# Attention scores by each head's own 64 rows, two weight granules multiplied unsplit, and six raw buffers, in a two-layer float32 decoder trunk

## The chip, the cores and the metric

The kernel runs on one core of one Trainium2 chip. The metric is the device time of one execution in microseconds (us). Three executions of the kernel before took 739.08, 737.74 and 739.0 us, so the median is 739.0 us.

TensorE multiplies: a weight load puts a stationary operand of up to 128 rows (the contraction) by 128 columns into the array, and a matmul streams a moving operand of up to 512 columns past it; sums go to PSUM banks. VectorE (DVE), ScalarE (ACT) and GpSimd (POOL) do the elementwise work, and SyncE's queue (SP) issues the DMA transfers, one after the other. Each engine executes its own instructions in the order of the program and waits on semaphores for the others.

## The reference, cut to what matters

One sequence of 256 tokens, 1024 features, passes two layers, all in float32. Per layer:

```python
proj = x @ w_in          # q,k,v of 8 stick-breaking heads | q,k,v of 8 MoBA heads | two gates
q_sb, k_sb, v_sb, q_mb, k_mb, v_mb, g_sb, g_mb = jnp.split(proj, cuts, axis=-1)
# stick-breaking, per head of 64 features:
z = jnp.einsum('bhqd,bhkd->bhqk', qi, k).astype(jnp.float32) * scale
log_keep = jnp.where(past, jax.nn.log_sigmoid(-z), 0.0)
suffix = lax.cumsum(log_keep, axis=3, reverse=True) - log_keep
w = jnp.where(past, jnp.exp(jax.nn.log_sigmoid(z) + suffix), 0.0)
# MoBA with rope on q and k; with 256 tokens only the own block is left: causal softmax
merged = jax.nn.sigmoid(g_sb) * branch_sb + jax.nn.sigmoid(g_mb) * branch_mb
x = layer_norm(DEEPNORM_ALPHA * x + merged @ w_out, ln_mix_g[l], ln_mix_b[l])
x = layer_norm(DEEPNORM_ALPHA * x + swiglu(x, w_gate, w_up, w_down), ln_ffn_g[l], ln_ffn_b[l])
```

In both kinds of attention a score is a product over the 64 features of one head, for each pair of a query and an earlier key.

## The kernel before, in words

**Precision.** Matmuls work on the type float32r, which keeps a part of float32's bits. To come near float32, each operand is split into a high part (a cast to float32r on ACT) and a low part (the rest, by a subtraction on DVE), and a product is three matmuls that add into one bank: high by high, high by low, low by high (`mm3`, line 334).

**Weights.** All weights come in granules of 128 by 1024 float32 (512 KB), 122 for each layer, in the order of their use. `WeightStream.load` (line 132) issues a granule's DMA into one of `NRAW` = 4 raw buffers; the first granule goes in two halves. `WeightStream.line` (line 143) casts it into a ring of ten granules (`whi`, ACT, line 162) and subtracts (`wlo`, DVE, line 166); then the raw buffer is free for a later granule, whose DMA the SP queue issues. `take` (line 175) hands a split granule to the matmuls.

**Order.** The order of all instructions is written out while the program is built. `Weave` keeps a planned time for TensorE (`weave.t`), ACT and DVE; a generator for a side task (splitting weights, a head pair's attention, rope) is stepped when the plan says that its next input is there. Each `mm` advances the plan by `max(n, 256) / 2400.0 + 0.002` us. The plan decides where a side task's matmuls and transposes stand among the others in TensorE's order; what really happens on the chip follows that order, whether inputs are there or not.

**Start.** Seven matmuls on zeros (`N_WARM`) are issued first. The input, transposed (`xT`), comes in eight pieces of 128 KB between the first granules, and is split into `xT_hi` and `xT_lo`. Layer 0 then begins with two projections of 128 tokens by 512 columns, twice each: values of the stick-breaking heads (`l0pv`, granules 0 to 3) and queries of the MoBA heads (`l0pq`, granules 4 to 7). `both_tokens` (line 368) runs them in an order of (token half, granule). Their sums stand in the two banks of pool `psM`. After `l0pq`, each token half goes through `rope_line`: a copy on ACT, rope on DVE, four transposes on TensorE (`l0qmb_tp`), and `put_qmb`.

**Scores.** Two heads make a pair: 64 rows each of one 128-row tile. For the queries, `stack_q` (line 401) makes a tile per head: its 64 rows hold the high part, the other 64 rows the low part. For the keys, `twice_k` (line 411) makes a tile per head with the high part in both halves, and another with the low part in the head's rows and zeros (a POOL memset) in the others. Then two matmuls over all 128 rows give a head's scores. The core of `scores` (line 449) is

```python
mm(o, q[h][:, p0 + j, qs], kh[h][:, p0 + j, ks], True, False)
mm(o, q[h][:, p0 + j, qs], kl[h][:, p0 + j, ks], False, True)
```

for two pairs, two heads and two query blocks (128 queries by 128 keys, 128 by 256): 16 matmuls in a group. There are four groups a layer (`sb0`, `sb1`, `mb0`, `mb1`), eight in all. The scores of a pair fill a tile of pool `psB` with one bank for each head; the transposed weights (`pT`) use the same pool, and `turnB` lets one line of attention at a time have it.

**Units.** Most large activations share `NACT` = 13 buffers of 4 KB a partition.

Of the kernel before, what the change touches and what calls it, by code (L numbers as in the profile page):

```python
# [31 lines left out]
EARLY = [*range(8), 8, 14, 9, 15, 20, 24, 21, 25, *range(10, 14), *range(16, 20), 22, 23, *range(26, 40)]  # L32
NACT = 13
NWIDE = 4
# [65 lines left out]
class WeightStream:  # L100
# [3 lines left out]
    def __init__(self, nc, pool, w, total, weave, rings):  # L104
        self.nc, self.pool, self.w, self.total, self.weave = nc, pool, w, total, weave
        self.loaded = self.split = 0
        self.done = -1
        self.current = 0
        self.rings = rings
        self._lay()  # L110
        self.dma_t = 1.7
        self.raw, self.parts, self.there, self.ready = {}, {}, {}, {}
# [14 lines left out]
    def _pieces(self, g):  # L127
        n = 2 if g == 0 else 1
        c = GCOLS // n
        return [slice(i * c, (i + 1) * c) for i in range(n)]  # L130

    def load(self, upto):
        while self.loaded < min(upto, self.total):
            g = self.loaded
            t = self.pool.tile([P, GCOLS], F32, tag="raw", name=f"raw{g}", bufs=NRAW)
            for sl in self._pieces(g):
                self.nc.sync.dma_start(t[:, sl], self.w[place(g), :, sl])
            self.raw[g] = t
# [45 lines left out]
RING = 10 * GCOLS + LINES  # L184
NRAW = 4
NSPLIT = 10
HOLD = 8
N_WARM = 7
LEAD = 2
# [21 lines left out]
def hybrid_trunk_kernel(ctx: ExitStack, tc: tile.TileContext, w, xT_in, x_in, ln_in,  # L211
# [57 lines left out]
    ident = const.tile([P, P], F32, name="ident")  # L269
    sb_kl = const.tile([P, 2, 2, S], F32R, name="sb_kl")  # L270
    ends = const.tile([P, 384], F32, name="ends")
    mask = const.tile([P, 2, P], F32, name="mask")
    warm = small.tile([P, 1], F32, tag="nmu", name="warm")

    nc.gpsimd.memset(sb_kl.bitcast(F32), 0.0)
    nc.gpsimd.memset(ends, 0.0)
# [11 lines left out]
    def load_xT(t, ks):  # L288
        nc.sync.dma_start(xT_raw[t][:, ks, :], xT_in[:, t, ks, :])
# [6 lines left out]

    kcs = [slice(k, k + 2) for k in range(0, KC, 2)]
    ws.side = weave.add(ws.line(), last=True)
    load_xT(0, kcs[0])
    ws.load(1)  # L300
    load_xT(1, kcs[0])
    for i in range(1, 4):
        load_xT(0, kcs[i])
        ws.load(i + 1)
        load_xT(1, kcs[i])
    split_xT(0, kcs[0])
    ws.take(0)
    split_xT(1, kcs[0])
    for i in range(1, 4):
        split_xT(0, kcs[i])  # L310
        if i < 3:
            ws.take(i)
        split_xT(1, kcs[i])
    weave.t = 4.5
# [12 lines left out]
    def mm(o, a, b, start, stop):  # L327
        nc.tensor.matmul(o, a, b, start=start, stop=stop)  # L328
        n = 1
        for d in b.shape[1:]:  # L330
            n *= d
        weave.t += max(n, 256) / 2400.0 + 0.002

# [21 lines left out]
    def split_to(hi, lo, src, n):  # L355
        return weave.start(split_line(hi, lo, src, n, pe_done()))

    def tok_major(o, g, t, first, last, k0):

        hi, lo = ws.take(g)  # L360
        hi = hi.rearrange("p (k c) -> p k c", k=2)
        lo = lo.rearrange("p (k c) -> p k c", k=2)
        for k in range(2):
            ts = slice(t * P, (t + 1) * P)
            mm3(o, xT_hi[:, k0 + k, ts], xT_lo[:, k0 + k, ts], hi[:, k, :], lo[:, k, :],
                first and k == 0, last and k == 1)

    def both_tokens(name, g0, put):

        acc = [bankM(f"{name}{t}", [P, WIDTH]) for t in range(2)]  # L370
        order = ((0, 0), (1, 0), (0, 1), (1, 1), (0, 2), (0, 3)) if g0 == 0 else \
            ((0, 0), (0, 1), (0, 2), (1, 0), (1, 1), (0, 3))
        for t, k in order + ((1, 2), (1, 3)):
            tok_major(acc[t], g0 + k, t, k == 0, k == 3, 2 * k)
            if t == 1:
                ws.used(g0 + k)
            if k == 3:
                put(t, acc[t])
# [17 lines left out]

    ROWS = [(slice(h * DH, (h + 1) * DH), slice((1 - h) * DH, (2 - h) * DH)) for h in range(2)]

    def stack_q(qs, src, n, c, e):

        for h, (a, b) in enumerate(ROWS):
            e = act(e, n, nc.scalar.activation, qs[h][a], src[a], AF.Copy, scale=c)
        yield e
        for h, (a, b) in enumerate(ROWS):
            e = dve(e, n, nc.vector.scalar_tensor_tensor, qs[h][b], src[a], c, qs[h][a].bitcast(F32),
                    op0=OP.mult, op1=OP.subtract)
        return e

    def twice_k(kh, kl, src, n, e):

        for h, (a, b) in enumerate(ROWS):
            e = act(e, n, nc.scalar.copy, kh[h][a], src[a])
        yield e
        e2 = e
        for h, (a, b) in enumerate(ROWS):
            e2 = dve(e2, n, nc.vector.tensor_sub, kl[h][a], src[a], kh[h][a].bitcast(F32))
            e = act(e, n, nc.scalar.copy, kh[h][b], kh[h][a].bitcast(F32))
        return max(e, e2)  # L420

# [26 lines left out]

    def scores(name, q, kh, kl, m, p0):
# [36 lines left out]
    def product_line(name, p, parts, v, oT, e, due):  # L486
# [19 lines left out]
        yield e  # L506
        for h, (a, b) in enumerate(ROWS):
            e = dve(e, S, nc.vector.tensor_add, both[a], o[:DH, h, :], low[:DH, h, :])
        yield e
        yield from split_line(oT[0][:, p, :], oT[1][:, p, :], both, S, e)  # L510

    def sb_line(name, d, q, q_there, ps, v, oT, done):

        kh = work.tile([P, 2, 2, S], F32R, tag="sbkh", name=f"{name}kh")
        kh, kl = ([x[:, h] for h in range(2)] for x in (kh, sb_kl))
# [5 lines left out]
        ss, es = yield from scores(name, q, kh, kl, 0, 0)  # L521
        ws_, fs = [], []
# [18 lines left out]

    def mb_line(name, d, q, kh, kl, v, oT, before, done, scored):
        while len(before) < 2:
# [4 lines left out]
        scored.append(name)  # L548
        ss, es = yield from scores(name, q, kh, kl, 1, 2 * d)
        work_, fs = [], []  # L550
# [111 lines left out]
    for l in range(DEPTH):  # L662
# [4 lines left out]
        v_sb = v_parts(L + "vsb")  # L667
        q_mb = [unit(f"{L}qmb{h}", [P, NPAIR, S], F32R) for h in range(2)]

        def put_qmb(tp, ts, e):  # L670
            return stack_q([q[:, :, ts] for q in q_mb], tp, WIDTH, 0.125, e)

# [30 lines left out]
        def sb_pairs(d, g):  # L703
            q = work.tile([P, 2, 2, S], F32R, tag="sbq", name=f"{L}sbq{d}")
            q, there = [q[:, h] for h in range(2)], [0.0]

            def q_line(ps):
                there[0] = 1e9
                there[0] = yield from stack_q(q, ps, WIDTH, 0.125, pe_done())
# [24 lines left out]
        sb_pairs(1, G + 12)  # L734
        k_mb = [[unit(f"{L}kmb{n}{h}", [P, NPAIR, S], F32R) for h in range(2)] for n in range(2)]
        for h, (a, b) in enumerate(ROWS):
            nc.gpsimd.memset(k_mb[1][h][b].bitcast(F32), 0.0)
# [9 lines left out]
        for d in range(2):  # L747
            sides.append(weave.add(mb_line(f"{L}mb{d}", d, q_mb, *k_mb, v_mb, o_mb, sigmoids, exps, scored)))
        for c in range(1, KC):
# [198 lines left out]
```

## Time and profile before

| what | before |
|---|---|
| median of three executions | 739.0 us |
| the profiled execution | 739.39 us |
| its span, first to last instruction | 737.4 us |
| PE busy | 724.9 us, 98% |
| PE weight loads busy | 670.1 us, 91% |
| DVE busy | 530.4 us, 72% |
| ACT busy | 408.0 us, 55% |
| DMA | 136.32 MB, mean 185 GB/s |

The profile is one execution. PE is TensorE's matmuls, PEld its weight loads, which run beside them. A row of a timeline gives the start and the duration in us, then engine, line, operation, output and inputs, the shape and how many were merged; brackets give the idle time before and what ended it. Matmuls overlap each other, so the pace of a stream is the distance of the starts, not the duration of one. Line L328 is the helper in which every matmul is issued, L341 the transposes', L51 and L56 the helpers of ACT and DVE, L137 the DMA of a granule.

### The profile page before, as it was taken

Reading aid. Unit: us, or ns where it says so; the run is one execution under the profiler, and the core shown is the slowest. Engines: PE = TensorE matmul, PEld = TensorE weight load, DVE = VectorE, ACT = ScalarE, POOL = GpSimd, SP = SyncE. Lnnn points to the kernel's source line nnn. Section 1 sums busy time; section 2 is a strip of 40 time slices with the busy share of each in tenths; the row PEclk is TensorE's granted clock in tenths of the full one; section 3 lists DMA queues with packets and bytes.
Section 4 is the critical chain, followed back from the end, with each engine's and each line's share of the span. In section 5 each row is a group of like instructions: output and inputs, shape, how many; then the busy total and the mean of one; then the engine's idle time right before and its main releaser. Section 6 shows DMA issues by size and latency. Waiting matters only on the chain.

```text
span 737.4 us, 12709 instructions
## 1 busy us (share of the span) xinstructions
PE 724.9 (98%) x5081; PEld 670.1 (91%) x5081; DVE 530.4 (72%) x740; ACT 408.0 (55%) x603; POOL 19.5 (3%) x35
## 2 busy tenths in 40 slices
PE   8999999999999999999999999999999999999996
PEld 6798899998799999988889989999988999999885
DVE  6798968796886666644479888778878866655416
ACT  6686767744565545534257856777446655444400
POOL 0001000000000000000000100000010000000001
PEclk9999999999999999999999999999999999999998
DMA  8874044775577555657167424448746855554701
GB/s 295 269 248 143 29 147 165 240 257 170 187 261 235 197 193 196 212 174 252 58 184 229 160 86 143 145 139 287 233 142 204 275 190 194 197 171 155 274 0 58
DMA packets 39082, 136.32 MB, mean 185 GB/s; under 512 B 4464, under 2 KB 6000, under 8 KB 39024
## 3 DMA queue, kind: packets, MB, share of 16 engines
q1 hardware_dynamic: 39024, 135.51, 55.5%
q8 instruction: 40, 0.66, 0.3%
q14 instruction: 18, 0.15, 0.1%
HBM read 134.45 MB, written 1.05 MB: 184 GB/s over the span
## 4 chain that ended last, share of the span: by engine, by line
PE 91%; DVE 3%; ACT 2%; DMA 2%; issue 1%; SPq 1%; POOL 1%; POOLq 0%; DVEq 0%; ACTq 0%
PE l1pf L328 13%; PE l0pf L328 13%; PE l0pd L328 8%; PE l1pg L328 6%; PE l0pg L328 5%; PE l1pe L328 4%; PE l1pd L328 4%; PE l1pk L328 3%; PE l0pk L328 3%; PE l1pvq L328 3%; PE l1pb L328 3%; PE l0pb L328 3%; PE l0pw L328 2%; PE l1pw L328 2%; PE l1pft L328 2%; PE l0pft L328 2%
## 5 line engine op out<-in xcount | busy, mean ns | idle before, releaser
L56 DVE TENSOR_TENSOR wlo<-raw,whi 128x1024 fp32r<-128x1024 f32 (+1 forms) x245 | 295.7, 1219 | 96.8 <-ACT whi L51 93.5
L51 ACT CAST whi<-raw 128x1024 fp32r<-128x1024 f32 (+1 forms) x245 | 253.3, 1046 | 84.5 <-DMA raw<-in_w_dram 38.4
L328 PE MATMUL l0pf<-xT_hi,whi 128*128 128x256 f32 x288 | 79.6, 276 | 0.0
L328 PE MATMUL l1pf<-xT_hi,whi 128*128 128x256 f32 x288 | 79.6, 276 | 0.0
L328 PE MATMUL l0pf<-xT_lo,whi 128*128 128x256 f32 x288 | 79.5, 276 | 0.0
L328 PE MATMUL l1pf<-xT_lo,whi 128*128 128x256 f32 x288 | 79.5, 276 | 0.0
L328 PE MATMUL l1pf<-xT_hi,wlo 128*128 128x256 f32 x288 | 79.5, 276 | 0.0
L328 PE MATMUL l0pf<-xT_hi,wlo 128*128 128x256 f32 x288 | 79.5, 276 | 0.0
L328 PEld LDWEIGHTS l0pf<-xT_lo,whi 128*128 128x128 f32 x288 | 54.1, 188 | 0.0
L328 PEld LDWEIGHTS l1pf<-xT_lo,whi 128*128 128x128 f32 x288 | 54.1, 188 | 0.0
L328 PEld LDWEIGHTS l0pf<-xT_hi,whi 128*128 128x128 f32 x288 | 54.1, 188 | 0.0
L328 PEld LDWEIGHTS l1pf<-xT_hi,whi 128*128 128x128 f32 x288 | 54.1, 188 | 0.0
L328 PEld LDWEIGHTS l1pf<-xT_hi,wlo 128*128 128x128 f32 x288 | 54.1, 188 | 0.0
L328 PEld LDWEIGHTS l0pf<-xT_hi,wlo 128*128 128x128 f32 x288 | 54.1, 188 | 0.0
L328 PE MATMUL l1pg<-xT_hi,whi 128*128 128x256 f32 x128 | 35.8, 279 | 0.0
L328 PE MATMUL l0pg<-xT_hi,whi 128*128 128x256 f32 x128 | 35.8, 279 | 0.0
L328 PE MATMUL l0pg<-xT_lo,whi 128*128 128x256 f32 x128 | 35.4, 276 | 0.0
L328 PE MATMUL l1pg<-xT_lo,whi 128*128 128x256 f32 x128 | 35.4, 276 | 0.0
L328 PE MATMUL l1pg<-xT_hi,wlo 128*128 128x256 f32 x128 | 35.4, 276 | 0.0
L328 PE MATMUL l0pg<-xT_hi,wlo 128*128 128x256 f32 x128 | 35.4, 276 | 0.0
L328 PE MATMUL l0pd<-whi,l0h_hi 128*128 128x512 f32 x88 | 34.4, 391 | 0.0
L328 PE MATMUL l0pd<-whi,l0h_lo 128*128 128x512 f32 x88 | 34.3, 389 | 0.0
(406 smaller groups left out, 1814.7 us busy)
## 6 DMA issues: line engine op xcount, KB each, us to landing
raw<-in_w_dram SPq DMA_DIRECT2D x243, 512.0 KB, 4.3
ln<-in_ln_dram SPq DMA_DIRECT2D x8, 512.0 KB, 6.0
xT_raw<-in_xT_dram SPq DMA_DIRECT2D x8, 128.0 KB, 5.1
x<-in_x_dram SPq DMA_DIRECT2D x2, 512.0 KB, 6.1
out_dram<-x SPq DMA_DIRECT2D x3, 256.0 KB, 2.0
raw<-in_w_dram SPq DMA_DIRECT2D x2, 256.0 KB, 3.3
out_dram<-x SPq DMA_DIRECT2D x2, 128.0 KB, 1.9
mask<-in_mask_dram SPq DMA_DIRECT2D x1, 128.0 KB, 4.0
```

The costliest lines, as they stand in the source:

```text
L51: f(*args, **kw)
L56: f(*args, **kw)
L328: nc.tensor.matmul(o, a, b, start=start, stop=stop)
```

## The change

Scores: queries and keys are split as everything else is, with both heads of a pair in one tile, high and low tiles apart. A head's score is three matmuls over its own 64 rows, and matmuls of the two heads alternate: 24 in a group. The stacked and doubled tiles, their extra ACT and DVE instructions and the POOL memsets go; the planner books a matmul over 64 rows at half.

Start: granules 0 and 1 are not split; `whole` multiplies raw float32 by raw float32, one matmul where there were three, eight matmuls in all. Granules 0 to 3 come in halves; `xT` comes in six pieces, the last two of 256 KB. There are six warm-up matmuls. The order of granules in both first projections is (0,0), (1,0), (0,1), (1,1), (0,2), (1,2), (0,3), (1,3), and the sums of the second stand in pool `psB`.

Buffers: `NRAW` goes from 4 to 6, `NACT` from 13 to 12.

```diff
-NACT = 13
+NACT = 12
-        self.loaded = self.split = 0
+        self.loaded, self.split = 0, NWHOLE
     def _pieces(self, g):
-        n = 2 if g == 0 else 1
+        n = 2 if g < 4 else 1
-NRAW = 4
+NRAW = 6
+NWHOLE = 2
+X_AFTER = {(0, 1): ((1, 0), (0, 1)), (1, 1): ((1, 1), (0, 2)), (2, 1): ((1, 2),)}
-N_WARM = 7
+N_WARM = 6
-    nc.gpsimd.memset(sb_kl.bitcast(F32), 0.0)
-    kcs = [slice(k, k + 2) for k in range(0, KC, 2)]
+    kcs = [slice(0, 2), slice(2, 4), slice(4, 8)]
...
+    def between(g, i):
+        for t, k in X_AFTER.get((g, i), ()):
+            load_xT(t, kcs[k])
+    ws.load(4, between)
...
-        weave.t += max(n, 256) / 2400.0 + 0.002
+        weave.t += (max(n, 256) / 2400.0 + 0.002) * a.shape[0] / P
...
+    def whole(o, g, t, first):
+        raw = ws.raw[g].rearrange("p (k c) -> p k c", k=2)
+        for k in range(2):
+            nc.tensor.matmul(o, xT_raw[t][:, 2 * g + k, :], raw[:, k, :], start=first and k == 0, stop=False)
+            weave.t += 4 * WIDTH / 2400.0
+            weave.tick()
     def tok_major(o, g, t, first, last, k0):
+        if g < NWHOLE:
+            return whole(o, g, t, first)
...
-        acc = [bankM(f"{name}{t}", [P, WIDTH]) for t in range(2)]
-        order = ((0, 0), (1, 0), (0, 1), (1, 1), (0, 2), (0, 3)) if g0 == 0 else \
-            ((0, 0), (0, 1), (0, 2), (1, 0), (1, 1), (0, 3))
-        for t, k in order + ((1, 2), (1, 3)):
+        acc = [banksB(f"{name}{t}")[:, 0, :] if g0 == 4 else bankM(f"{name}{t}", [P, WIDTH]) for t in range(2)]
+        order = ((0, 0), (1, 0), (0, 1), (1, 1), (0, 2), (1, 2), (0, 3)) if g0 <= 4 else \
+            ((0, 0), (0, 1), (0, 2), (1, 0), (1, 1), (0, 3), (1, 2))
+        for t, k in order + ((1, 3),):
...
+    ROWS = [slice(h * DH, (h + 1) * DH) for h in range(2)]
+    def scaled_line(hi, lo, src, n, c, e):
+        e = act(e, n, nc.scalar.activation, hi, src, AF.Copy, scale=c)
         yield e
+        return dve(e, n, nc.vector.scalar_tensor_tensor, lo, src, c, hi.bitcast(F32), op0=OP.mult, op1=OP.subtract)
...
-            for h in range(2):
-                for c0, qs, ks in ((0, slice(0, P), slice(0, P)), (P, slice(P, S), slice(0, S))):
-                    o = s[:, h, c0:c0 + ks.stop]
-                    mm(o, q[h][:, p0 + j, qs], kh[h][:, p0 + j, ks], True, False)
-                    mm(o, q[h][:, p0 + j, qs], kl[h][:, p0 + j, ks], False, True)
+            for qs, ks in ((slice(0, P), slice(0, P)), (slice(P, S), slice(0, S))):
+                for n, (a, b) in enumerate(((0, 0), (0, 1), (1, 0))):
+                    for h, r in enumerate(ROWS):
+                        mm(s[:, h, qs.start:qs.start + ks.stop], q[a][r, p0 + j, qs], k[b][r, p0 + j, ks],
+                           n == 0, n == 2)
...
-        e = yield from twice_k(kh, kl, ps, WIDTH, pe_done())
+        e = yield from split_line(*k, ps, WIDTH, pe_done())
...
-            return stack_q([q[:, :, ts] for q in q_mb], tp, WIDTH, 0.125, e)
+            return scaled_line(*(q[:, :, ts] for q in q_mb), tp, WIDTH, 0.125, e)
...
-        k_mb = [[unit(f"{L}kmb{n}{h}", [P, NPAIR, S], F32R) for h in range(2)] for n in range(2)]
-        for h, (a, b) in enumerate(ROWS):
-            nc.gpsimd.memset(k_mb[1][h][b].bitcast(F32), 0.0)
+        k_mb = pair_tiles(f"{L}kmb", [P, NPAIR, S])
-            yield from twice_k(*([k[:, :, ts] for k in part] for part in k_mb), tp, WIDTH, e)
+            return split_line(*(k[:, :, ts] for k in k_mb), tp, WIDTH, e)
```

More of the change, by code (lines that the diff above doesn't have):

```diff
@@ L127, in _pieces, with load @@
     def _pieces(self, g):
-        n = 2 if g == 0 else 1
+        n = 2 if g < 4 else 1
         c = GCOLS // n
         return [slice(i * c, (i + 1) * c) for i in range(n)]
-    def load(self, upto):
+    def load(self, upto, between=lambda g, i: None):
         while self.loaded < min(upto, self.total):
@@ L135, in load @@
             t = self.pool.tile([P, GCOLS], F32, tag="raw", name=f"raw{g}", bufs=NRAW)
-            for sl in self._pieces(g):
+            for i, sl in enumerate(self._pieces(g)):
                 self.nc.sync.dma_start(t[:, sl], self.w[place(g), :, sl])
+                between(g, i)
             self.raw[g] = t
@@ L269, in hybrid_trunk_kernel @@
     ident = const.tile([P, P], F32, name="ident")
-    sb_kl = const.tile([P, 2, 2, S], F32R, name="sb_kl")
     ends = const.tile([P, 384], F32, name="ends")
@@ L295, in split_xT @@
         dve(e, n, nc.vector.tensor_sub, xT_lo[:, ks, t * P:(t + 1) * P], xT_raw[t][:, ks, :], hi.bitcast(F32))
-    kcs = [slice(k, k + 2) for k in range(0, KC, 2)]
+    kcs = [slice(0, 2), slice(2, 4), slice(4, 8)]
     ws.side = weave.add(ws.line(), last=True)
     load_xT(0, kcs[0])
[L300 to L313, printed above, removed]
+    def between(g, i):
[3 more added lines that the diff above has]
+    for k in range(2):
+        for t in range(2):
+            split_xT(t, kcs[k])
+    for k in range(4, KC, 2):
+        split_xT(0, slice(k, k + 2))
+        ws.take(k // 2)
+        split_xT(1, slice(k, k + 2))
     weave.t = 4.5
@@ L356, in split_to @@
         return weave.start(split_line(hi, lo, src, n, pe_done()))
+    def whole(o, g, t, first):
+        raw = ws.raw[g].rearrange("p (k c) -> p k c", k=2)
+        for k in range(2):
+            nc.tensor.matmul(o, xT_raw[t][:, 2 * g + k, :], raw[:, k, :], start=first and k == 0, stop=False)
+            weave.t += 4 * WIDTH / 2400.0
+            weave.tick()
     def tok_major(o, g, t, first, last, k0):
+        if g < NWHOLE:
+            return whole(o, g, t, first)
         hi, lo = ws.take(g)
@@ L395, in token_out @@
             mm3(ps, s_hi[:, ts], s_lo[:, ts], hi[:, cs], lo[:, cs], first, last)
-    ROWS = [(slice(h * DH, (h + 1) * DH), slice((1 - h) * DH, (2 - h) * DH)) for h in range(2)]
-    def stack_q(qs, src, n, c, e):
-        for h, (a, b) in enumerate(ROWS):
-            e = act(e, n, nc.scalar.activation, qs[h][a], src[a], AF.Copy, scale=c)
+    ROWS = [slice(h * DH, (h + 1) * DH) for h in range(2)]
+    def scaled_line(hi, lo, src, n, c, e):
+        e = act(e, n, nc.scalar.activation, hi, src, AF.Copy, scale=c)
         yield e
[L406 to L420, printed above, removed]
+        return dve(e, n, nc.vector.scalar_tensor_tensor, lo, src, c, hi.bitcast(F32), op0=OP.mult, op1=OP.subtract)
     def rope_line(name, ps, t, put):
@@ L447, in hybrid_trunk_kernel, with scores @@
     PARTS = ((0, P), (P, 384))
-    def scores(name, q, kh, kl, m, p0):
+    def scores(name, q, k, m, p0):
         ss = [banksB(f"{name}_s{j}") for j in range(2)]
         for j, s in enumerate(ss):
-            for h in range(2):
-                for c0, qs, ks in ((0, slice(0, P), slice(0, P)), (P, slice(P, S), slice(0, S))):
-                    o = s[:, h, c0:c0 + ks.stop]
-                    mm(o, q[h][:, p0 + j, qs], kh[h][:, p0 + j, ks], True, False)
-                    mm(o, q[h][:, p0 + j, qs], kl[h][:, p0 + j, ks], False, True)
+            for qs, ks in ((slice(0, P), slice(0, P)), (slice(P, S), slice(0, S))):
[3 more added lines that the diff above has]
+                           n == 0, n == 2)
         e = pe_done()
@@ L506, in product_line @@
         yield e
-        for h, (a, b) in enumerate(ROWS):
-            e = dve(e, S, nc.vector.tensor_add, both[a], o[:DH, h, :], low[:DH, h, :])
+        for h, r in enumerate(ROWS):
+            e = dve(e, S, nc.vector.tensor_add, both[r], o[:DH, h, :], low[:DH, h, :])
         yield e
@@ L512, in sb_line @@
     def sb_line(name, d, q, q_there, ps, v, oT, done):
-        kh = work.tile([P, 2, 2, S], F32R, tag="sbkh", name=f"{name}kh")
-        kh, kl = ([x[:, h] for h in range(2)] for x in (kh, sb_kl))
-        e = yield from twice_k(kh, kl, ps, WIDTH, pe_done())
+        k = work.tile([P, 2, 2, S], F32R, tag="sbk", name=f"{name}k")
+        k = [k[:, n] for n in range(2)]
+        e = yield from split_line(*k, ps, WIDTH, pe_done())
         e = max(e, q_there[0])
@@ L520, in sb_line @@
         pe_after(e)
-        ss, es = yield from scores(name, q, kh, kl, 0, 0)
+        ss, es = yield from scores(name, q, k, 0, 0)
         ws_, fs = [], []
@@ L540, in sb_line, with mb_line @@
         yield from weighted(name, d, [beta for _, beta in ws_], v, oT, es)
-    def mb_line(name, d, q, kh, kl, v, oT, before, done, scored):
+    def mb_line(name, d, q, k, v, oT, before, done, scored):
         while len(before) < 2:
@@ L548, in mb_line @@
         scored.append(name)
-        ss, es = yield from scores(name, q, kh, kl, 1, 2 * d)
+        ss, es = yield from scores(name, q, k, 1, 2 * d)
         work_, fs = [], []
@@ L667, in hybrid_trunk_kernel @@
         v_sb = v_parts(L + "vsb")
-        q_mb = [unit(f"{L}qmb{h}", [P, NPAIR, S], F32R) for h in range(2)]
+        q_mb = pair_tiles(f"{L}qmb", [P, NPAIR, S])
         def put_qmb(tp, ts, e):
-            return stack_q([q[:, :, ts] for q in q_mb], tp, WIDTH, 0.125, e)
+            return scaled_line(*(q[:, :, ts] for q in q_mb), tp, WIDTH, 0.125, e)
         ropes = []
@@ L704, in sb_pairs @@
             q = work.tile([P, 2, 2, S], F32R, tag="sbq", name=f"{L}sbq{d}")
-            q, there = [q[:, h] for h in range(2)], [0.0]
+            q, there = [q[:, n] for n in range(2)], [0.0]
             def q_line(ps):
                 there[0] = 1e9
-                there[0] = yield from stack_q(q, ps, WIDTH, 0.125, pe_done())
+                there[0] = yield from scaled_line(*q, ps, WIDTH, 0.125, pe_done())
             for n, name in enumerate("qk"):
@@ L734, in hybrid_trunk_kernel @@
         sb_pairs(1, G + 12)
-        k_mb = [[unit(f"{L}kmb{n}{h}", [P, NPAIR, S], F32R) for h in range(2)] for n in range(2)]
-        for h, (a, b) in enumerate(ROWS):
-            nc.gpsimd.memset(k_mb[1][h][b].bitcast(F32), 0.0)
+        k_mb = pair_tiles(f"{L}kmb", [P, NPAIR, S])
         def put_kmb(tp, ts, e):
-            yield from twice_k(*([k[:, :, ts] for k in part] for part in k_mb), tp, WIDTH, e)
+            return split_line(*(k[:, :, ts] for k in k_mb), tp, WIDTH, e)
         both_tokens(f"{L}pk", G + 16, lambda t, ps: ropes.append(weave.start(rope_line(L + "kmb", ps, t, put_kmb))))
@@ L747, in hybrid_trunk_kernel @@
         for d in range(2):
-            sides.append(weave.add(mb_line(f"{L}mb{d}", d, q_mb, *k_mb, v_mb, o_mb, sigmoids, exps, scored)))
+            sides.append(weave.add(mb_line(f"{L}mb{d}", d, q_mb, k_mb, v_mb, o_mb, sigmoids, exps, scored)))
         for c in range(1, KC):
```

## The prediction

> **What bounds the kernel.** I read the page first, then the chain of waits in order of time, then timelines of the start and of two stretches of attention, and last the rows of single tiles.
>
> ```profile
> span 737.4 us, 12709 instructions
> ...
> PE 724.9 (98%) x5081; PEld 670.1 (91%) x5081; DVE 530.4 (72%) x740; ACT 408.0 (55%) x603; POOL 19.5 (3%) x35
> ...
> PE 91%; DVE 3%; ACT 2%; DMA 2%; issue 1%; SPq 1%; POOL 1%; POOLq 0%; DVEq 0%; ACTq 0%
> ```
>
> The chain that ended last is TensorE for 91%. So a change can win in two ways only: fewer TensorE slots, or fewer of the stalls that hold TensorE. ACT and DVE have room almost everywhere. The chain in order of time shows both (start, length, what, xcount):
>
> ```profile
> 6.71 6.36 DMA xT_raw<-in_xT_dram
> ...
> 22.78 6.12 DMA raw<-in_w_dram
> 28.98 1.05 ACT whi L51
> ...
> 32.18 0.63 PE l0qmb_tp L341 x4
> ...
> 48.67 1.85 PE l0sb_s L328 x16
> ...
> 106.57 1.32 PE l0mb_pT L341 x12
> ...
> 213.64 95.90 PE l0pf L328 x846
> 309.54 55.11 PE l0pd L328 x243
> ```
>
> From 33 us on the chain is TensorE with short breaks; until then it also runs through transfers and ACT. A stream of matmuls with 256 moving columns has a pace of 95.90 / 846 = 0.113 us, with 512 columns 55.11 / 243 = 0.227 us. A group of scores takes 1.85 / 16 = 0.116 us a matmul, although half of its matmuls have only 128 columns. Which limit that is, the timeline of a product with both widths tells, matmuls and then weight loads:
>
> ```profile
> 114.25 0.28 PE L328 MATMUL l0mb_o<-l0mb_plo,l0vmb 128*128 128x256 f32 x1
> 114.37 0.22 PE L328 MATMUL l0mb_o<-l0mb_phi,l0vmb 128*128 128x128 f32 x1
> 114.43 0.28 PE L328 MATMUL l0mb_o<-l0mb_plo,l0vmb 128*128 128x128 f32 x1
> 114.54 0.33 PE L328 MATMUL l0mb_o<-l0mb_phi,l0vmb 128*128 128x256 f32 x1
> ```
>
> ```profile
> 114.25 0.19 PEld L328 LDWEIGHTS l0mb_o<-l0mb_phi,l0vmb 128*128 128x128 f32 x1
> 114.37 0.19 PEld L328 LDWEIGHTS l0mb_o<-l0mb_plo,l0vmb 128*128 128x128 f32 x1
> 114.48 0.19 PEld L328 LDWEIGHTS l0mb_o<-l0mb_phi,l0vmb 128*128 128x128 f32 x1
> ```
>
> Two matmuls of 128 columns start 0.06 us apart (114.37, 114.43), but the next has to wait, and the loads start every 0.11 to 0.12 us whatever the width. The transposes, 128 columns each, go at 1.32 / 12 = 0.110 us. So the scores are **bound by weight loads**, one 128-column load at about 0.115 us for each matmul.
>
> **The change, part by part.**
>
> *Scores.* A group goes from 16 loads and matmuls of 128 rows to 24 of 64 rows, the two heads in turn. No row of this trace has a load over 64 rows, so I bound it. If loads of the two halves run beside each other, a group is 12 slots: 12 x 0.116 = 1.39 us, a gain of 0.46 us, 3.7 us over eight groups. If each load takes the slot of a whole one, it is 24 x 0.116 = 2.78 us, a loss of 0.93, 7.4 us in all. If a half load also takes half the time, matmuls bind: 6 x 0.06 + 6 x 0.113 = 1.04 us, a gain of 6.5 us. I take the first. The loads above last 0.19 us and start every 0.115, so the load path has two under way already, and the two heads read different partitions, fill different rows and add into different banks. Nothing in the trace proves it.
>
> The array also turns from 128 rows to 64 and back: 16 switches. The nearest row is the turn from matmuls to transposes, which go at 0.110 us from the first one, so it may be free; at most a switch lets the last matmul run out (0.28 - 0.113 = 0.17 us) and hides no load (0.19 us), 0.36 us, 5.8 us in all. I take 0.08 us a switch, 1.3 us: nearer to the free row. Scores net: -3.7 + 1.3 = **-2.4 us**.
>
> The Trainium skill, "TensorEngine Tiling (Array Packing)", Key Properties, says that tiles can load weights and multiply in parallel, but that a change of the tiling mode drains TensorE. By the first the gain of 3.7 stands, by the second the upper price of a switch; no row of before shows either. The Trainium skill, "TensorE: Matmul & The Clock Gate", LDWEIGHTS (loading the stationary operand), says that a load's time follows its columns and not its rows; that speaks against the gain of 6.5 us and, if loads queue up one by one, for the loss.
>
> *Splits of queries and keys.* What goes, and the form of 128 rows by which it is replaced:
>
> ```profile
> L51 ACT CAST l0kmb<-l0kmb_tp x4: 580/580/584, 74.2 to 81.3; 64x512 fp32r<-64x512 f32 x4
> L51 ACT CAST l0kmb<-l0kmb x4: 615/620/620, 75.3 to 83.4; 64x512 fp32r<-64x512 f32 x4
> L56 DVE TENSOR_TENSOR l0kmb<-l0kmb_tp,l0kmb x4: 675/688/695, 79.0 to 82.6; 64x512 fp32r<-64x512 f32 x4
> L737 POOL MEMSET l0kmb<- x2: 948/952/956, 55.3 to 56.3; 64x1024 f32 x2
> ```
>
> ```profile
> L51 ACT CAST l0vsb<-l0pv x2: 587/588/588, 17.2 to 20.0; 128x512 fp32r<-128x512 f32 x2
> L56 DVE TENSOR_TENSOR l0vsb<-l0pv,l0vsb x2: 680/686/692, 17.9 to 20.6; 128x512 fp32r<-128x512 f32 x2
> ```
>
> 128 rows cost what 64 do. Four key splits a layer lose three ACT and one DVE instruction each, four query splits one of each: 16 x 0.59 = 9.4 us of ACT and 8 x 0.69 = 5.5 us of DVE a layer. TensorE's stream covers all of it (ACT is 55% busy), so I book nothing but for the stall at 112 us. There `l0mb_s` waits for `l0mb_plo`, queued on DVE behind weight splits (waits from 107 to 114.5 us):
>
> ```profile
> PEld l0mb_s L328 <- DVE l0mb_plo L56: 1.0, 1, 1.0
> ```
>
> That is 1.0 us, once, and the chain has no such piece in layer 1. With other buffers and less work the queue will stand otherwise; the gain is 0 to 1.0 us, and a stall of that size can as well appear elsewhere (+1.0). I take **-0.4 us**. Without that room on ACT and DVE each saved instruction would count 0.6 to 0.7 us.
>
> *Start.* The timeline of the first 20 us:
>
> ```profile
> 4.42 1.27 ACT L51 CAST whi<-raw 128x512 fp32r<-128x512 f32 x2 [0.64 <-DMA raw<-in_w_dram]
> ...
> 5.09 0.80 PE L328 MATMUL l0pv<-whi,xT_hi 128*128 128x512 f32 x1 [0.24 <-ACT whi L51]
> ...
> 8.54 0.63 PE L328 MATMUL l0pv<-wlo,xT_hi 128*128 128x512 f32 x1
> ...
> 8.97 0.63 PE L328 MATMUL l0pv<-whi,xT_lo 128*128 128x512 f32 x1
> ...
> 9.76 0.40 PE L328 MATMUL l0pv<-wlo,xT_hi 128*128 128x512 f32 x1
> ...
> 9.99 0.40 PE L328 MATMUL l0pv<-whi,xT_lo 128*128 128x512 f32 x1
> ...
> 11.40 1.23 DVE L56 TENSOR_TENSOR wlo<-raw,whi 128x1024 fp32r<-128x1024 f32 x1
> ...
> 15.77 0.50 PE L328 MATMUL l0pv<-wlo,xT_hi 128*128 128x512 f32 x1 [0.61 <-DVE wlo L56]
> ```
>
> ```profile
> 19.76 0.39 PE L328 MATMUL l0pq<-whi,xT_hi 128*128 128x512 f32 x1
> ```
>
> The pace is 0.43 us before 9.4 us and 0.23 after: TensorE runs at half clock first. A `whole` matmul needs only landed data, so the first starts at about 4.45 us (the cast's release) in place of 5.09. No row has a float32 matmul; the planner books 4 x 512 / 2400 = 0.853 us for it. The low end is one pass, 0.23 us; the high end is four at half clock, 4 x 0.43 = 1.71 us. I take the planner's figure, doubled until 9.4: three matmuls to 9.57, five more to 13.84, then 24 at 0.227 us to 19.29. Granule 2's high part is there by then (its DVE split was made at 11.40 to 12.63), and the 0.61 us stall before 15.77 goes, since DVE splits two granules fewer. So `l0pv` ends at 19.3 against 19.76: **-0.5 us**. At full clock from the first matmul it would wait for granule 2's low part at 12.6 and end at 17.8 (-2.0); at half clock through all eight, at 23.6 (+3.8).
>
> *Six raw buffers.* The stall before `l0qmb_tp` is the largest of the front:
>
> ```profile
> 30.41 0.39 PE L328 MATMUL l0pq<-whi,xT_lo 128*128 128x512 f32 x1
> ...
> 32.18 0.63 PE L341 MATMUL l0qmb_tp<-ident,l0qmb_tok 128*128 128x128 f32 x4 [1.38 <-ACT whi L51]
> ```
>
> One slot after 30.41 is 30.64, so 1.54 us are lost. ACT copies `l0pq` for rope only after a cast that sat waiting for a granule issued at 22.78, because its raw buffer was not free earlier:
>
> ```profile
> SPq L137 <- DVE wlo L56: 23.0, 16, 3.1
> ```
>
> ```profile
> ACT whi L51 <- DMA raw<-in_w_dram: 3.5, 1, 3.5
> ```
>
> The first row is the SP queue's waits up to 46 us, the second ACT's from 28 to 34. Two more buffers let a transfer be issued two splits earlier, and two granules are never split: for granule 11 that is 22.78 - 4 x 1.23 = 17.9, and with its 6.1 us it lands at about 24 in place of 28.9. But granules 6 and 7 now wait for TensorE to finish granules 0 and 1 (about 10.4 and 13.8 us by the working above), and granule 8 and the three small late loads queue behind them on SP. The plan may then pull casts further ahead and wait for granule 14 or 15 instead, so of 1.54 us I take **-1.1 us** (0 to -1.5). The sums in `psB` free both `psM` banks for the next projection; its first scores come 18 us later (48.67), so nobody waits for them.
>
> **Sum.** The profiled execution is 739.4 us by its own time (span 737.4 and 2.0 around it), 0.4 above the median of 739.0. 739.4 - 2.4 - 0.4 - 0.5 - 1.1 = **735.0 us**.
>
> **Rivals.**
>
> *One load at a time.* The two heads' loads pass one path, each at 0.116 us: +7.4 us in the eight groups, -2.0 elsewhere: 744.8 us. For it: every load of the trace, wide or narrow product, keeps that slot. Against it: loads overlap in time. It makes the kernel slower from a pair of loads taking over 0.155 + 0.02 us (16 x 0.116 / 12 and the other gains spread over 96 pairs) and decides at the first group near 48 us. It is also the case in which the change does not do what it says.
>
> *Costly switches.* The heads run side by side, but each of 16 switches costs 0.36 us: -3.7 + 5.8 - 2.0 = 739.5 us, no change. Against it stand the transposes' free turns. It is what the drain of "TensorEngine Tiling (Array Packing)" in the Trainium skill would give at its dearest.
>
> *Half clock through the unsplit matmuls:* +3.8 in place of -0.5: 739.3 us. Against it: dense work had brought the clock up at 9.4 us, and the new start has fewer holes.
>
> *Half loads at half price:* -6.5 + 1.3 - 2.0 = 732.2 us. Nothing in the trace speaks for it.
>
> **Numbers.** The forecast gets 0.66, one load at a time 0.20, costly switches 0.07, half clock 0.04, half price 0.03. About 0.2% (1.5 us) is what a measurement of this kernel can tell from no change. Faster is the forecast but for its edge, and half price: 0.69; no change is both 739 us cases and that edge: 0.12; slower is one load at a time almost alone: 0.19. The forecast's own range is 732 to 738, from its unknowns (a switch 0 to 0.17 us, the start -2.0 to +1.0, the two stalls 0 to -2.5 together). For 8 in 10 the range is 731.5 to 742: it takes in the 739 us cases and the mild end of one load at a time.
>
> **What would show it.** Right: a group of scores from its first matmul to the next work takes 1.4 to 1.6 us, with starts of the two heads in pairs; `l0pq` begins at 18 to 19.5 us; no gap over 0.5 us before `l0qmb_tp`. Wrong: 24 loads at 0.11 us each in a group (one at a time), a gap at its edges (switches), a pace of 1.7 us beyond 9.4 us (clock), or a new wait of ACT for a granule ahead of the copy of `l0pq`.

## The result, and the profile after

| what | before | after |
|---|---|---|
| median | 738.12 us, 737.66 to 739.08, 6 executions | 734.21 us, 734.05 to 735.36, 6 executions |
| ratio after / before, 95% interval | | 0.9949, 0.9936 to 0.9962 |
| the profiled execution, its span | 739.39 us, 737.4 | 734.21 us, 732.4 |
| TensorE's share of the chain that ended last | 91% | 95% |

The kernel is 0.5% faster: 3.9 us by the medians, 5.2 by the two profiled executions (that of before, 739.39, lies above its six others, so the two profiles show about 1 us more than the medians). 735.0 us was forecast. So the sum was right; its terms were not, as the marks below show.

The page of after, its span, the busy times and the chain by engine:

```profile
span 732.4 us, 12739 instructions
...
PE 723.1 (99%) x5136; PEld 664.7 (91%) x5136; DVE 515.6 (70%) x723; ACT 384.5 (52%) x570; POOL 14.8 (2%) x30
...
PE 95%; DVE 2%; issue 1%; ACT 1%; POOL 1%; POOLq 0%; DVEq 0%
```

From 1.5 us on, nothing but TensorE is left in the chain up to the first layer norm (176 us). The chain of after in order of time (start, length, what, xcount):

```profile
4.42 7.61 PE l0pv L362 x16
12.04 5.45 PE l0pv L328 x24
17.49 12.18 PE l0pq L328 x57
29.67 0.44 PE l0qmb_tp L341 x4
...
35.18 5.44 PE l0pk L328 x48
...
103.84 4.10 PE l0pg L328 x36
107.94 1.57 PE l0mb_s L328 x24
...
137.94 21.76 PE l0pb L328 x192
...
365.45 6.81 PE l1pvq L328 x30
...
443.65 6.01 PE l1pg L328 x51
...
463.29 4.24 PE l1pg L328 x36
...
497.52 21.76 PE l1pb L328 x192
```

The rows of the chain of before that answer to it:

```profile
38.81 5.44 PE l0pk L328 x48
...
113.11 1.19 PE l0mb_s L328 x8
...
142.85 21.76 PE l0pb L328 x192
...
370.34 6.81 PE l1pvq L328 x30
...
448.77 5.78 PE l1pg L328 x51
...
502.43 21.76 PE l1pb L328 x192
```

The starts of the same piece in both are marks on TensorE's way; what the distance grows from one to the next is what the stretch between them gained. The first matmul of `l0pq` was at 19.76 before; after it is the last row of this timeline of after:

```profile
4.22 7.81 PE L362 MATMUL l0pv<-raw,xT_raw 128*128 128x512 f32 x16
...
17.33 0.39 PE L328 MATMUL l0pq<-whi,xT_hi 128*128 128x512 f32 x1
```

| mark | before | after | stretch gained |
|---|---|---|---|
| first matmul of `l0pq` | 19.76 | 17.33 | 2.43 |
| `l0pk` | 38.81 | 35.18 | 1.20 |
| `l0pb` | 142.85 | 137.94 | 1.28 |
| `l1pvq`, layer 1 | 370.34 | 365.45 | -0.02 |
| `l1pb` | 502.43 | 497.52 | 0.02 |
| span | 737.4 | 732.4 | 0.09 |

Layer 0 has the whole gain. Layer 1, with four of the eight groups of scores but none of the stalls, has nothing: 132.09 us from `l1pvq` to `l1pb` before, 132.07 after. So what was won are holes, not slots. The rows of `l1pg` show where layer 1 loses again what its groups save: the 51 matmuls ahead of the first `l1mb_s` group took 5.78 us before and take 6.01 after. The 1.28 us between `l0pk` and `l0pb` are mostly the stall at 112 us, 1.15 us with its edges. Before, the group of scores there was broken in two by `l0mb_plo`; after, all 24 matmuls stand in one piece of 1.57 us.

**A group of scores.** Timelines of the first `l0mb_s` group, matmuls of before and then of after:

```profile
93.55 0.28 PE L328 MATMUL l0pg<-xT_hi,wlo 128*128 128x256 f32 x1
93.66 2.01 PE L328 MATMUL l0mb_s<-l0kmb,l0qmb 128*128 128x128 f32 x16
95.51 0.28 PE L328 MATMUL l0pg<-xT_hi,whi 128*128 128x256 f32 x1
95.63 0.28 PE L328 MATMUL l0pg<-xT_lo,whi 128*128 128x256 f32 x1
```

```profile
89.93 0.28 PE L328 MATMUL l0pg<-xT_hi,wlo 128*128 128x256 f32 x1
90.14 0.33 PE L328 MATMUL l0mb_s<-l0kmb_hi,l0qmb_hi 64*128 64x128 f32 x2
90.30 0.28 PE L328 MATMUL l0mb_s<-l0kmb_lo,l0qmb_hi 64*128 64x128 f32 x2
...
91.50 0.28 PE L328 MATMUL l0mb_s<-l0kmb_hi,l0qmb_lo 64*128 64x256 f32 x2
91.71 0.38 PE L328 MATMUL l0pg<-xT_hi,whi 128*128 128x256 f32 x1
91.93 0.28 PE L328 MATMUL l0pg<-xT_lo,whi 128*128 128x256 f32 x1
```

The weight loads of the same stretch of after:

```profile
89.81 0.19 PEld L328 LDWEIGHTS l0pg<-xT_hi,wlo 128*128 128x128 f32 x1
90.14 0.18 PEld L328 LDWEIGHTS l0mb_s<-l0kmb_hi,l0qmb_hi 64*128 64x128 f32 x2
90.25 0.19 PEld L328 LDWEIGHTS l0mb_s<-l0kmb_lo,l0qmb_hi 64*128 64x128 f32 x2
```

Two loads make one row (x2), start 3 to 4 ns apart and together last hardly longer than one did; the next pair starts 0.11 us later. So the heads' loads do run side by side, 12 slots in place of 16. But from the last `l0pg` ahead of the group to the second one behind it are 95.63 - 93.55 = 2.08 us before and 91.93 - 89.93 = 2.00 after. Of 4 x 0.116 = 0.46 us only 0.08 arrived. Three distances at the edges have grown from 0.11 or 0.12 to 0.21 or 0.22 (89.93 to 90.14, 91.50 to 91.71, 91.71 to 91.93), and the 11 steps inside take 1.37 us, 0.09 more than 11 x 0.116. That is 0.38 us for two switches, **0.19 us each**. The load rows fit this: before the group of the old kind its first load starts at 93.55, together with the last `l0pg` matmul; here no load runs ahead of the switch (none starts between 89.81 and 90.14). From the last matmul ahead to the fourth behind, the mean over the four groups of layer 1 is 2.415 us before and 2.334 after, and the unbroken groups of layer 0 take the same: 0.65 us for eight groups.

### The profile page after: what moved, and what is told of

It reads as the page before. It is cut to its first block, busy times and chain, and to the rows that moved or that the text cites. A ratio compares the mean times of both kernels' runs of the same rounds, so it can differ in the third digit from the quotient of the medians.

```text
span 732.4 us, 12739 instructions
## 1 busy us (share of the span) xinstructions
PE 723.1 (99%) x5136; PEld 664.7 (91%) x5136; DVE 515.6 (70%) x723; ACT 384.5 (52%) x570; POOL 14.8 (2%) x30
## 4 chain that ended last, share of the span: by engine, by line
PE 95%; DVE 2%; issue 1%; ACT 1%; POOL 1%; POOLq 0%; DVEq 0%
PE l1pf L328 13%; PE l0pf L328 13%; PE l0pd L328 8%; PE l1pg L328 6%; PE l0pg L328 6%; PE l1pe L328 4%; PE l1pd L328 4%; PE l0pq L328 3%; PE l0pk L328 3%; PE l1pk L328 3%; PE l1pvq L328 3%; PE l1pb L328 3%; PE l0pb L328 3%; PE l1pw L328 2%; PE l0pw L328 2%; PE l0pft L328 2%
## 5 line engine op out<-in xcount | busy, mean ns | idle before, releaser
L56 DVE TENSOR_TENSOR wlo<-raw,whi 128x1024 fp32r<-128x1024 f32 (+1 forms) x244 | 292.1, 1214 | 77.1 <-ACT whi L51 74.2
L51 ACT CAST whi<-raw 128x1024 fp32r<-128x1024 f32 (+1 forms) x244 | 249.8, 1042 | 68.4 <-PE l0pd L328 19.1
```

The lines of the kernel that those rows point to most:

```text
L51: f(*args, **kw)
L56: f(*args, **kw)
```

## Experiments

The theory after this reading: the gain is buffers and the new start; the scores' side-by-side loads are real, but two switches a group eat them. The rivals: the scores free the gain through ACT and DVE (the stalls went because work went), and the switch is not the price at the edges.

### The scores alone, on the kernel before

```diff
-    mm(o, q[h][:, p0 + j, qs], kh[h][:, p0 + j, ks], True, False)
-    mm(o, q[h][:, p0 + j, qs], kl[h][:, p0 + j, ks], False, True)
+    for n, (a, b) in enumerate(((0, 0), (0, 1), (1, 0))):
+        for h, r in enumerate(ROWS):
+            mm(..., q[a][r, p0 + j, qs], k[b][r, p0 + j, ks], n == 0, n == 2)
```

with the splits, the tiles and the planner's half price that belong to it; start and buffers as before.

> The kernel before with the new scores alone (queries and keys split plainly, three matmuls over each head's own 64 rows); start, orders and four raw buffers as before. Theory A, from the trace after: a group of scores costs 12 slots of 0.115 us and two switches of 0.19 us, 2.34 us where it was 2.43 with its neighbours, so eight groups give 0.7 us; the 1.4 us stall ahead of the first rope transposes stays, and the 1.0 us stall at 112 us may go or stay: 0.7 to 1.8 us faster than before. Theory B, the prediction's term: switches are cheap in total and the scores give 2.4 us by themselves.

Measured: 739.66 us against 738.49, ratio 1.0018 (1.0007 to 1.0029). Neither theory held. The groups cost what they cost in after (2.334 us), the stall at 112 us is gone, and so is that before the first `l0qmb_tp`; 0.46 us are left before the second. Still the kernel isn't faster, for a stall that neither kernel has. Its row in TensorE's waits from 50 to 62 us, and the chain that leads to it:

```profile
PEld l0pk L326 <- DVE l0sbq L56: 2.1, 1, 2.1
```

```profile
40.55 1.23 DVE wlo L56
41.80 5.66 DMA raw<-in_w_dram
...
57.06 0.69 DVE l0sbq L56
57.80 2.67 PE l0pk L326 x6
```

A granule lands at 47.5, late: its raw buffer came free only with the split that ended at 41.8. Its own cast and split then stand ahead of the scores' steps in the queues of ACT and DVE, and 10 us later `l0sbq` is late for TensorE. Six matmuls of 512 columns then take 2.67 us in place of 6 x 0.227 = 1.36: the granted clock had fallen, as a stretch of this kernel shows (from and to, us, PE, PEld, DVE, ACT, POOL busy, PEclk, DMA share, GB/s):

```profile
58.10:61.50 3.40, 3.40 (x12) 2.77 (x11) 1.37 (x2) 0.00 (x0) 0.00 (x0) 0.50 0.31 73
```

So the 2.06 us without a matmul were followed by 3.4 us at half clock, about 1.7 us more. This is one execution, of 740.71 us. The twelve lie between 737.47 and 741.59 us, those of before between 737.42 and 739.37: five have 740.7 or more, the other seven a median of 738.6, level with before. So the 0.2% are not a fixed price, and whether all executions have this stall isn't shown. Less work on ACT and DVE didn't take the stalls away as a whole.

The front of this kernel shows one thing more. Up to 33 us its instructions on TensorE, ACT and DVE, its raw buffers and its transfers are those of before. But the granule that took 6.12 us to land in the profile of before (issued at 22.78) took 4.43 here (issued at 23.05), ACT's cast waited 1.63 us for it in place of 3.54, and the first rope transposes were not held. The stall at 32 us is thus not in every execution of those instructions: between these two it goes with the time of one transfer.

### One more buffer alone, on the kernel before

```diff
-NACT = 13
+NACT = 12
-NRAW = 4
+NRAW = 5
```

> The kernel before with five raw buffers (and 12 units), nothing else. By theory C, that late transfers hold ACT and DVE, the 1.4 us stall ahead of the first rope transposes shrinks and the kernel is 0.5 to 1.5 us faster. Rival: with the old start and the old scores ACT and DVE are late for themselves, and a buffer more does nothing (within 0.3 us) or moves the stall elsewhere.

Measured: 736.93 us against 739.06, ratio 0.9974 (0.9965 to 0.9984). The chain of this kernel:

```profile
20.30 10.88 PE l0pq L328 x48
31.18 0.44 PE l0qmb_tp L341 x4
...
110.70 1.85 PE l0mb_s L328 x16
```

Both stalls are gone: `l0qmb_tp` follows `l0pq` at once, and the group at 110.70 is in one piece, with the old scores and the old start. A fifth buffer alone brings half of the gain, 2.1 us, more than the 0.5 to 1.5 expected.

### The scores with six buffers, old start

The kernel of the first experiment with

```diff
-NACT = 13
+NACT = 12
-NRAW = 4
+NRAW = 6
```

> New scores and six raw buffers (12 units) with the start and the orders of before. Theory C, formed after the first four runs: the buffers carry the change, because the stalls at 30 to 35 and at 55 us are ACT and DVE standing behind a late transfer; with six buffers they go, and what is left against the changed kernel is the start, 0.5 to 1.5 us slower than it. Rival: the unsplit granules free ACT and DVE early and carry it; then the stalls stay and the time is 737.5 us or more, as with the scores alone.

Measured: 736.68 us against 738.71, ratio 0.9975 (0.9966 to 0.9984). All stalls between 30 us and the first layer norm are gone. What is left against after are 2.2 us (0.5 to 1.5 were expected), and they are the start; TensorE's waits from 4 to 17 us in this kernel:

```profile
PEld l0pv L326 <- ACT whi L51: 2.4, 2, 1.6
PEld l0pv L326 <- DVE wlo L56: 2.3, 3, 1.1
```

`l0pq` begins at 19.86 us. 0.9975 with the new scores against 0.9974 with the old ones and one buffer fewer: once buffers are there, the new scores are worth nothing that can be measured, as in layer 1.

### The change with four and with five raw buffers

```diff
-NRAW = 6
+NRAW = 4
```

> The changed kernel with four raw buffers in place of six. Theory A: the stall ahead of the first rope transposes was one of late transfers, so with four buffers most of its 1.4 us comes back: 1.0 to 1.5 us slower than the changed kernel. Rival: granules that are no longer split and the earlier start took the stall away, and two more buffers are worth nothing: same time as the changed kernel within 0.3 us.

Measured: 737.65 us against 738.49, ratio 0.9991 (0.9981 to 1.0002), no difference from before. TensorE's waits from 26 to 60 us:

```profile
PEld l0pk L328 <- DVE l0sbq L56: 1.5, 1, 1.5
PEld l0qmb_tp L341 <- ACT whi L51: 1.1, 1, 1.1
```

These are the stall of before at `l0qmb_tp` and that of the scores alone, in one kernel. It is over 3 us slower than the changed kernel, twice what theory A expected, and its rival falls. Without the buffers the change wins nothing that is certain.

```diff
-NRAW = 6
+NRAW = 5
```

> The changed kernel with five raw buffers, the control for the run with the old scores and five. If five are enough, no stall over 0.5 us at 30 and 55 us and the time of the changed kernel within 0.5 us; then the 4.5 us that the old scores lost belong to the scores, their splits and their booking in the plan. If five are as bad as four, about 3 us slower, and the old scores by themselves lost only about 1 us.

Measured: 735.39 us against 739.06, ratio 0.9955 (0.9942 to 0.9967). A stall of 0.36 us at 30.8 and one of 0.22 at 31.9 are left. The fifth buffer carries nearly all, the sixth some half a microsecond, and the intervals of both kernels overlap.

### The old scores in the new kernel

Six raw buffers don't fit beside the stacked tiles, so this one has five:

```diff
-NRAW = 6
+NRAW = 5
-    mm(..., q[a][r, p0 + j, qs], k[b][r, p0 + j, ks], n == 0, n == 2)
+    mm(o, q[h][:, p0 + j, qs], kh[h][:, p0 + j, ks], True, False)
+    mm(o, q[h][:, p0 + j, qs], kl[h][:, p0 + j, ks], False, True)
```

> The changed kernel with the scores of before (stacked queries, doubled keys, 16 matmuls over 128 rows, the old booking in the plan), and five raw buffers because six do not fit beside the larger tiles. Theory A: the start keeps its gain, the scores lose 0.7 us: 0.7 us slower than the changed kernel, about 1.8 if the stall at 112 us comes back with the longer splits. Theory B: 2.4 us slower or more.

Measured: 738.91 us against 738.49, ratio 1.0006 (0.9996 to 1.0015). By the number that is theory B; but the groups are only back at 2.415 us, 0.65 us in all, so its mechanism is not what the trace shows. The rest of the 3.5 us to the kernel with five buffers (3.8 by the ratios) doesn't lie in the groups: the trace has stalls of 1.27 and 0.92 us at 101 to 103 us, where `l0pg` waits for `whi` behind `l0mb_e` on ACT and then for `wlo`, and 0.65 at 31. The plan came out otherwise with the old scores' instructions and put a weight split behind a softmax. 0.65 and 2.84 less the 0.58 us of the stalls of five buffers are 2.9; 0.6 to 0.9 us are not settled. So with this start the exchange of the scores costs what the change wins, by one place in the order; whether another order would give it back was not tried.

### The start, split again

```diff
-NWHOLE = 2
+NWHOLE = 0
```

with granules 0 and 1 split between the splits of `xT` in the preamble; pieces and order of the transfers as in the change.

> The changed kernel with granules 0 and 1 split as all others are (three matmuls for one); six buffers, pieces of transfers and new scores stay. Theory A: the unsplit matmuls make the start: the first one waits for ACT again, TensorE has holes in the first 6 us, its clock comes up near 9.4 us in place of 5.3, and the second projection starts 2 to 2.5 us later than the 17.3 us of the changed kernel. Rival: the gain of the start came from the order and the pieces of the transfers: less than 0.7 us later, since the split form needs 1.4 us less of TensorE at full clock.

Measured: 735.37 us against 738.49, ratio 0.9962 (0.9949 to 0.9974). In its timeline `l0pq` starts at

```profile
17.88 0.39 PE L331 MATMUL l0pq<-whi,xT_hi 128*128 128x512 f32 x1
```

That is 0.55 us behind after and 1.88 ahead of before, whose start it would be if the unsplit matmuls were the cause. Behind the second of its 48 matmuls there isn't one wait for a split. Two kernels with the unsplit matmuls in which the clock came up at 7.6 us (the one with switches added in the middle, and the one with the old scores) began `l0pq` later than this one, at 18.24 and 18.32. So most of the new start is the order and the pieces of the transfers (and buffers that let them go out), not the matmuls left unsplit; a share of up to a microsecond for these can't be told from the clock's own moment, which came at 8.7 us here.

### What a switch costs

Three matmuls of 128 rows and 128 columns are added in each group, into columns of a bank that nobody reads. In one kernel they stand between the blocks of the group, six switches more; in the other at its end, none more.

```diff
+                if (j, qs.start) != (1, P):
+                    mm(ss[j][:, 0, 384:], xT_hi[:, 0, :P], xT_hi[:, 0, :P], True, True)
```

> The changed kernel with three matmuls over 128 rows added in each group of scores, one after each of the first three blocks (128 columns each, into bank columns that nobody reads): three slots of 0.115 us and six switches more a group. With 0.19 us a switch a group is 0.35 + 1.14 us longer, eight groups 11.9 us; with the prediction's 0.08 us 6.6 us; with its upper price of 0.36 us 20 us.

```diff
+        for _ in range(3):
+            mm(ss[1][:, 0, 384:], xT_hi[:, 0, :P], xT_hi[:, 0, :P], True, True)
```

> The control: the same three added matmuls all at the end of a group, so that no switch is added: 0.35 us a group, 2.8 us in all.

Measured: 747.09 us, ratio 1.0111 (1.0097 to 1.0125), and 739.38 us, ratio 1.0006 (0.9997 to 1.0015), both against 739.06. The first `l0mb_s` group between the blocks, and then at the end:

```profile
94.49 0.28 PE L328 MATMUL l0pg<-xT_hi,wlo 128*128 128x256 f32 x1
...
95.18 0.33 PE L328 MATMUL l0mb_s<-xT_hi 128*128 128x128 f32 x1
95.44 0.39 PE L328 MATMUL l0mb_s<-l0kmb_hi,l0qmb_hi 64*128 64x256 f32 x2
...
97.76 0.28 PE L328 MATMUL l0pg<-xT_lo,whi 128*128 128x256 f32 x1
```

```profile
91.54 0.28 PE L328 MATMUL l0pg<-xT_hi,wlo 128*128 128x256 f32 x1
...
93.32 0.55 PE L328 MATMUL l0mb_s<-xT_hi 128*128 128x128 f32 x3
...
93.88 0.28 PE L328 MATMUL l0pg<-xT_lo,whi 128*128 128x256 f32 x1
```

97.76 - 94.49 = 3.27 us against 93.88 - 91.54 = 2.34: 0.93 us for six switches, **0.155 us each**. The medians say the same over 48 switches: 7.71 / 48 = 0.16. The same instructions in another order cost 7.7 us, so it is the switch that is paid for, not the instructions. (Both kernels also lose 1.16 us ahead of `sb_o` in each layer, 2.3 us that the expectations didn't have. So the first kernel's 12 to 13 us over after agree with the expected 11.9 partly by luck: its groups account for 10.1. The second's 4.4 to 5 us are 2.7 of its groups and these 2.3.)

### The order inside a group

Twice the order was changed: all three matmuls of one head ahead of the other's three, and the wide block ahead of the narrow one.

```diff
-                for n, (a, b) in enumerate(((0, 0), (0, 1), (1, 0))):
-                    for h, r in enumerate(ROWS):
+                for h, r in enumerate(ROWS):
+                    for n, (a, b) in enumerate(((0, 0), (0, 1), (1, 0))):
```

> The changed kernel with the order inside a group of scores turned: three matmuls of one head, then three of the other, in place of the two heads in turn; same 24 matmuls. If matmuls and loads over different rows overlap only with their neighbour in the order, a group has 17 slots in place of 12, 0.58 us more, and the kernel is 4.6 us slower than the changed one. If the loads run ahead freely, nothing changes. If nothing overlaps, 24 slots: 11 us slower.

```diff
-            for qs, ks in ((slice(0, P), slice(0, P)), (slice(P, S), slice(0, S))):
+            for qs, ks in ((slice(P, S), slice(0, S)), (slice(0, P), slice(0, P))):
```

> The changed kernel with the two query blocks of a pair in the other order, the 256-column products first, so that a group ends with 128 columns: the last matmul before the switch back is 0.05 us shorter, a group 2.29 in place of 2.34 us, 0.4 us in all, if what a switch costs is the run-out of the last matmul.

The change itself ran beside them:

> The changed kernel itself, beside the others of this call. 0.995 of the kernel before, no stall of TensorE over 0.5 us between the start and the first layer norm. The clock turned to full at 5.3 us in its first profile, and at 5.9 and 7.7 us in two kernels with the same start: if that moment is free of the kernel, it lies elsewhere here too, between about 5 and 10 us, and the second projection starts up to 1.5 us later than 17.3.

Measured, against 738.71: heads apart 734.69, ratio 0.9949 (0.9936 to 0.9961); blocks swapped 734.34, ratio 0.9943 (0.993 to 0.9955); the change once more 734.48, ratio 0.9946 (0.9933 to 0.996). With the heads apart a group takes 2.340 us, 0.006 more, which is next to no difference, and the timeline has the same rows, the first of them:

```profile
90.10 0.33 PE L328 MATMUL l0mb_s<-l0kmb_hi,l0qmb_hi 64*128 64x128 f32 x2
```

The two matmuls in this row are first and fourth in the program; the trace has them 10 ns apart, where one place in the order made 3 to 4 ns. With the blocks swapped a group takes 2.29 us, 0.05 less, as expected for a narrow block next to the switch; over eight groups that is 0.4 us, less than the intervals can tell. None of these versions is known to beat the change.

## Why the prediction was right in its sum and not in its terms

| step | forecast | measured | by |
|---|---|---|---|
| loads side by side | -3.7 | true: pairs 3 to 4 ns apart, 12 slots | loads of after |
| 16 switches | +1.3 (0.08 each) | +2.5 to +3.0 (0.155 by the experiment, 0.19 by the edges) | group edges; switches in the middle against the end |
| scores, groups in all | -2.4 | -0.65 | eight groups, 2.415 to 2.334 |
| stall at 112 us | -0.4 | -1.15 | chain of after |
| start, to `l0pq` | -0.5 | -2.43 | timeline |
| stall before `l0qmb_tp` | -1.1 | -1.2 from `l0pq` to `l0pk` | chain |

That the sum came to the forecast is luck: the scores gave 1.75 us less than booked and the start 1.9 more. The range of 732 to 738 had room for both.

**The step that failed is the price of a switch**: "nearer to the free row" took the turn to transposes as its likeness. That turn stays at 128 rows; a turn to 64 rows is another thing, and the first load waits for it. 0.19 us lies in the middle of the bounds, 0 to 0.36. The Trainium skill, "TensorEngine Tiling (Array Packing)", Key Properties, says that a change of the tiling mode drains TensorE; the 0.155 us by which six switches differ from none agree with it. And the -0.65 us at the groups don't reach the end: in layer 1, where only the scores changed and no stall stood, the two kernels are level to 0.02 us. What is given back is seen in two stretches: the 51 matmuls of `l1pg` ahead of the first `l1mb_s` group take 6.01 us in place of 5.78, and the 36 ahead of the second 4.24 where the same 36 of layer 0 take 4.10. That is 0.37 us, as much as four groups save. All kernels here with the new scores have the 6.01, in layer 0 too, and the three with the old ones have the 5.78, whatever their buffers and start. Why the pace there is 0.118 and not 0.113 us is not settled.

**The start was under-estimated** at one assumption: half clock until 9.4 us, as before. In after most of the unsplit matmuls ran at full clock, by the group of their records (two for each matmul; ns min/median/max, first and last start), and by five of them in the timeline:

```profile
L362 PE MATMUL l0pv<-raw,xT_raw x16: 592/592/1115, 4.2 to 11.4; 128*128 128x512 f32 x16
```

```profile
9.73 2.31 PE L362 MATMUL l0pv<-raw,xT_raw 128*128 128x512 f32 x5
```

Most have the short duration, 592 ns, and five of them start (2.31 - 0.59) / 4 = 0.43 us apart, which is 0.86 us for a matmul. The eight take 7.61 us from 4.42, 0.73 more than 8 x 0.86, against 9.4 in the working (4.45 to 13.84). The granted clock turned to full at 5.3 us in this execution, so half clock held for some 1 us of them; the (9.4 - 5.3) / 2 = 2.1 us so saved are about the 1.96 by which the working (19.29) came out late. The 24 split matmuls behind them came at 0.227 us each as forecast, to 17.33. The planner's 0.853 us for one is right at full clock. And that moment isn't fixed by the kernel: full clock came at 5.3 and 6.3 us in two executions of after, and between 4.7 and 9.7 us over 14 profiled executions. With the old start that moment hardly counts: `l0pq` began at 19.76 with the clock at 9.7 and at 19.86 with the clock at 6.2, where the rows above show waits for `whi` and `wlo`. With the new one it does: 17.05 to 18.32, so 1.4 to 2.7 us ahead of before. The measured -2.43 lies beyond the forecast's low bound, -2.0, which saw the wrong limit there: granule 2's low part was in time.

**The stalls** went as forecast in the front, with some luck: the -1.2 us are the distance to one execution of before, in which one transfer took 6.12 us, and another execution with the same front had no such stall. That buffers matter rests on the medians (one buffer alone, and four against five and six in the changed kernel). For the stall at 112 us the runs don't separate two reasons: a buffer alone removes it with the old scores; the two kernels with the new scores and four buffers don't have it either, but each has another stall near 56 us, of 2.06 and 1.5 us. "A stall of that size can as well appear elsewhere" was the right warning, with too small a price.

**The rivals.** One load at a time falls with the pairs of loads. Costly switches had half of its price in it: at 0.36 us the scores would have lost 2.1, at 0.19 they are worth nearly nothing. Half clock through the unsplit matmuls was refuted by their median of 592 ns. Half loads at half price falls too: a load of 64 rows has 0.18 to 0.19 us, as one of 128.

By the runs the gain is about 1.9 us of buffers (one buffer alone 0.9974), 2.2 us of start (736.68 to 734.48) and, with enough buffers and the old start, nothing measurable of scores, the title's first item. What the old scores would be worth with the new start in a better order is open.

## What to carry to other kernels

Where engines execute in order, a transfer that is late by one buffer holds a cast, the cast holds a softmax, and TensorE pays 10 us later: try one more buffer alone before any rewriting of the work, and look for the moved stall when work goes away. Halves of the array do run side by side, but each turn into and out of that mode costs about 0.16 to 0.19 us here, so 12 slots in place of 16 pay only if many slots stand between two turns. Time each part alone and with its companions: here the scores were 0.2% slower alone by the median, level with buffers, and a total that agreed with its forecast hid two terms that were wrong by nearly 2 us each.

## What the runs showed of the hardware

- A switch between 128 and 64 rows costs 0.155 to 0.19 us, and no weight load runs ahead across it in these traces (89.81 to 90.14 without one).
- The two row halves are two streams. With the heads apart in the program, the second head's first matmul starts 10 ns after the first head's by the trace, ahead of two matmuls that precede it in the program. The Trainium skill, "TensorE: Matmul & The Clock Gate", Part 3, states that matmuls start and end strictly in program order; these rows differ.
- A hole of 2.06 us on TensorE was followed by a granted clock of 0.50 for 3.4 us in one execution; holes of 1.54 us or less, as that of before at 32 us, were not.
- A float32 matmul of 512 columns takes 0.86 us at full clock and is shown as two records 0.43 us apart.
